# Encoder layer with retrieved experts: the low part of the one-hot weights on ScalarE in every second group, and a larger share for gathered rows

## Chip, cores and metric

The kernel runs on one core of a Trainium2 chip. The metric is the device time of one execution in microseconds (us). The engines carry their profile names: PE (TensorE), PEld (its weight loads), DVE (VectorE), ACT (ScalarE), POOL (GpSimd), SP (SyncE, which here issues transfers).

## What is computed

One layer of an encoder, 512 tokens of width 1024: an attention half and a recurrent half, then the retrieval of experts, then a gated embedding and a norm. The edit lies in the retrieval. Each token has 8 heads with 16 experts each, 128 of 16384, chosen by two short key searches; an expert is a row of `exp_u` and a row of `exp_v`:

```
idx, g = top 16 of the key sums, softmax of their scores    # per token and head
ue = exp_u[idx];  logits = einsum('td,tkd->tk', x, ue)
act = gelu(logits) * g
ve = exp_v[idx];  out = einsum('tk,tkd->td', act, ve)
```

## The kernel before, in words

The tokens form four tiles of 128. Three of them take the dense way: the products of all 16384 rows of `u` with the 384 tokens are formed on PE (the u product, 128 steps of 128 experts), gelu is applied, and the result is multiplied by a weight matrix that holds g at the chosen experts and zero elsewhere, and then with all rows of `v` (the v product, 128 steps again). The fourth tile takes the sparse way: for each of its tokens' 128 experts POOL gathers 128 rows (one for each token) from `u`, DVE forms dot products (L926), and later POOL gathers rows of `v` and DVE adds them to `h` (L933). That makes 256 gathers, called rows here.

Products run on 32-bit words split in a high part (by ACT, L89) and a low part (by DVE, L91), three matmuls for each product (L96 to L98). `row_load` loads and splits a block of rows, three blocks ahead of PE; `u_mm` (L655 on) forms 24 matmuls into one of two PSUM banks `psl`, which ACT empties with gelu (L660). In the v product six banks `acc` collect the sums.

The weight matrix is made by `build`, for one tile of 128 tokens, in groups of eight. For each group `hot` makes one-hot tiles on DVE: `o1` and `m2` compare a count from 0 to 127 with the first and second key's number (L830, one instruction of 1024 f16 elements each), and two multiplications put the weight on `m2`: `o2` with its high part and, in place, `m2` with its low part (L835). PE multiplies the two one-hot tiles of each token, high and low, into a bank `pg` (L855, 16 matmuls a group), ACT copies that to `sg` (L858), and every two groups `sg` is written to memory (`gd`, L860). A group's one-hot tiles are made one group ahead. For the second branch of `hot`, which the kernel before never takes since HOT_DVE is 4, ACT makes the same product in eight activations, one for each token, with the weight as the scale.

The order is set by hand. The loop over the 128 steps of the u product calls three generators after each step, each with a share: `top` (key search, tile by tile, the sparse tile first), `make` (the builds, a share of 0.5, a group costs 1.0) and `side` (the rows; one costs 1.15). `side` gets SIDE_1 while the first dense tile's indices are unknown, SIDE until all builds are done, then SIDE_2. At step 122 the builds that are left are forced, and `settle` opens the room of the v product and loads the first weights back from memory. In the loop of the v product the rows get BG_V at each step, or the last weights are prepared instead. Rows that are left come after the last step (`bg.run(1e9)`), together with `finish`: norm, turn, gate product and output of each tile (L1133 to L1165). The gathered rows' tile is the last to finish, since its `h` needs all rows. The order in which each engine gets its instructions follows from these calls and from a scheduler that interleaves what is ready. Every gather waits for the newest split of a block (`pace`).

Of the kernel before, what the change touches and what calls it, by code (L numbers as in the profile page):

```python
# [39 lines left out]
KEEP = 26  # L40
G_SCALE = 2.0 ** 14
RO_AT = [2, 1, 1, 1, 1, 1, 1, 0, 0, 1, 0, 0, 1, 0, 0, 1, 0, 0, 1, 1, 9]
TOP_FIRST, TOP_THEN, MAKE, SIDE_1, SIDE, BG_V, HOT_DVE, PREP, SIDE_2 = 2.2, 1.0, 0.5, 0.6, 1.2, 1.2, 4, 60, 2.1
LAST = 3
N_HOT = 13
N_AT = 15, 17, 17
# [1256 lines left out]
```

## Time and profile before

| | |
|---|---|
| median of 3 runs | 1504.44 us (1502.62 to 1505.04) |
| profiled execution | 1502.74 us, span 1501.0 us |
| PE, DVE, ACT, POOL busy | 98%, 84%, 49%, 29% of the span |
| u product | about 295 to 895 us |
| builds of the weights | about 400 to 866 us |
| v product | about 898 to 1437 us |

A row of a view gives an engine, a line of the kernel, the operation, the tiles (written <- read), the shape, and a count after x. Behind the bar stand busy us, mean ns of one, and the idle time of the engine just before, with what ended it. In a timeline the columns are start, duration, engine, line, operation; in brackets, idle time and what ended it. In a table of stretches the engines stand in the order PE, PEld, DVE, ACT, POOL, then the granted clock of PE (1.00 is full speed), the share of the DMA engines and GB/s.

### The profile page before, as it was taken

How to read it: one execution, taken by the hardware profiler on the slowest of the kernel's cores; microseconds unless marked ns; L12 is line 12 of the kernel's file. 1: busy time of each engine (PE TensorE's matmuls, PEld its weight loads, DVE VectorE, ACT ScalarE, POOL GpSimd, SP SyncE). 2: the span in 40 equal slices, each digit the busy share in tenths (PEclk: the TensorE clock that was granted, in tenths of full speed). 3: DMA queues.
4: the chain of work that ended last, by engine and by line, in shares of the span. 5: the costliest groups of instructions: out<-in, count | busy, mean ns of one | idle time of the engine just before them, and what ended most of it. 6: DMA issues, size and time to landing. Idle time of an engine off the chain costs nothing.

```text
span 1501.0 us, 22206 instructions
## 1 busy us (share of the span) xinstructions
PE 1464.1 (98%) x7907; PEld 1294.7 (86%) x7907; DVE 1257.0 (84%) x2481; ACT 741.1 (49%) x1059; POOL 428.6 (29%) x320
## 2 busy tenths in 40 slices
PE   8999999999899999999999989999999999999996
PEld 6887678899899999999999987888888888888875
DVE  7686987789999999999878757788887588878895
ACT  7974754354555654565455533333333453333345
POOL 0000000010223374235333344344443014344450
PEclk9999999999999999999999999999999999999998
DMA  7223022156789898889998799989999789999971
GB/s 257 61 94 127 15 86 88 43 195 229 239 294 335 285 347 327 305 296 345 370 330 300 266 321 340 321 300 328 360 373 359 248 280 351 366 353 357 322 227 64
DMA packets 169199, 394.21 MB, mean 263 GB/s; under 512 B 15360, under 2 KB 90880, under 8 KB 166016
## 3 DMA queue, kind: packets, MB, share of 16 engines
q1 hardware_dynamic: 112336, 207.52, 41.1%
q0 software_dynamic: 38464, 140.00, 26.4%
q10 hardware_dynamic: 18288, 45.27, 7.8%
q8 instruction: 62, 1.02, 0.3%
q14 instruction: 49, 0.40, 0.1%
HBM read 345.41 MB, written 47.32 MB: 262 GB/s over the span
## 4 chain that ended last, share of the span: by engine, by line
PE 66%; DVE 21%; ACT 4%; issue 4%; DMA 3%; SPq 1%; DVEq 0%; ACTq 0%
PE acc L98 11%; PE acc L97 11%; PE acc L96 11%; PE psl L96 6%; PE psl L97 6%; PE psl L98 6%; DVE rl L91 4%; PE pg L855 2%; DVE rr L926 2%; PE ps L96 2%; PE ps L98 2%; PE ps L97 2%; DVE h L933 1%; DMA r<-in_v_dram 1%; SPq L1000 1%
## 5 line engine op out<-in xcount | busy, mean ns | idle before, releaser
L89 ACT ACTIVATE rh<-r 128x1024 fp32r<-128x1024 f32 x256 | 270.8, 1059 | 423.1 <-PE psl L97 188.1
L91 DVE TENSOR_TENSOR rl<-r,rh 128x1024 fp32r<-128x1024 f32 x256 | 312.2, 1220 | 95.5 <-ACT rh L89 93.4
L96 PE MATMUL psl<-x2h,rh 128*128 128x384 f32 x1024 | 348.2, 340 | 7.4 <-ACT keep L660 5.0
L98 PE MATMUL psl<-x2h,rl 128*128 128x384 f32 x1024 | 344.3, 336 | 3.6 <-DVE rl L91 3.6
L97 PE MATMUL psl<-x2l,rh 128*128 128x384 f32 x1024 | 343.9, 336 | 0.0
L98 PE MATMUL acc<-rh,al 128*128 128x512 f32 x768 | 299.8, 390 | 1.1 <-DVE al L91 1.1
L96 PE MATMUL acc<-rh,ah 128*128 128x512 f32 x768 | 299.4, 390 | 0.7 <-ACT ah L89 0.7
L97 PE MATMUL acc<-rl,ah 128*128 128x512 f32 x768 | 299.4, 390 | 0.3 <-DVE rl L91 0.3
L894 POOL DMA_INDIRECT rr<-in_u_dram,qidx x84 | 123.0, 1465 | 382.0 <-DVE rl L91 180.7
L894 POOL DMA_INDIRECT rr<-in_v_dram,qidxv x82 | 150.8, 1839 | 187.7 <-DVE rl L91 163.9
L96 PEld LDWEIGHTS psl<-x2h,rh 128*128 128x128 f32 x1024 | 193.0, 189 | 8.9 <-ACT keep L660 5.3
L98 PEld LDWEIGHTS psl<-x2h,rl 128*128 128x128 f32 x1024 | 193.2, 189 | 4.6 <-DVE rl L91 4.5
L97 PEld LDWEIGHTS psl<-x2l,rh 128*128 128x128 f32 x1024 | 193.3, 189 | 0.0
L98 PEld LDWEIGHTS acc<-rh,al 128*128 128x128 f32 x768 | 144.5, 188 | 31.8 <-DVE al L91 1.9
L96 PEld LDWEIGHTS acc<-rh,ah 128*128 128x128 f32 x768 | 144.6, 188 | 31.2 <-ACT ah L89 1.1
L97 PEld LDWEIGHTS acc<-rl,ah 128*128 128x128 f32 x768 | 144.4, 188 | 30.6 <-DVE rl L91 0.7
L89 ACT ACTIVATE ah<-am 128x384 fp32r<-128x384 f32 x128 | 66.3, 518 | 94.9 <-DVE am L1057 61.5
L933 DVE SCALAR_TENSOR_TENSOR h<-rr,qg,h 128x1024 f32<-128x1024 f32 x82 | 104.9, 1279 | 3.7 <-DMA rr<-in_v_dram,qidxv 3.7
L926 DVE CUSTOM_DVE_ANT_0 rr<-rr,xn 128x1024 f32<-128x1024 f32 x84 | 102.1, 1217 | 6.0 <-DMA rr<-in_u_dram,qidx 6.0
L894 POOL DMA_INDIRECT xn<-in_u_dram,qidx x44 | 68.6, 1559 | 110.7 <-DVE rl L91 92.7
L894 POOL DMA_INDIRECT xn<-in_v_dram,qidxv x46 | 74.8, 1627 | 88.8 <-DVE rl L91 81.4
L858 ACT COPY sg<-pg 128x512 f32<-128x512 f32 x96 | 95.8, 1107 | 1.0 <-ACT sc L695 0.4
(342 smaller groups left out, 2275.5 us busy)
## 6 DMA issues: line engine op xcount, KB each, us to landing
r<-in_ut_dram SPq DMA_DIRECT2D x128, 512.0 KB, 4.8
r<-in_v_dram SPq DMA_DIRECT2D x128, 512.0 KB, 6.8
gd<-sg ACTq DMA_DIRECT2D x24, 1024.0 KB, 7.5
gc<-gd SPq DMA_DIRECT2D x128, 192.0 KB, 7.7
ld<-lg ACTq DMA_DIRECT2D x102, 192.0 KB, 5.0
lg<-ld SPq DMA_DIRECT2D x102, 192.0 KB, 6.3
w<-in_w_qkv_dram SPq DMA_DIRECT2D x12, 512.0 KB, 3.6
w<-in_w_out_dram SPq DMA_DIRECT2D x8, 512.0 KB, 3.8
```

What stands on the lines that cost most here:

```text
L89: nc.scalar.activation(hi, src, AF.Copy, scale=1.0 if scale is None else scale)
L91: return nc.vector.tensor_sub(lo, src, hi.bitcast(F32))
L96: nc.tensor.matmul(ps, lhsT=lh, rhs=rh, start=first, stop=False)
L97: nc.tensor.matmul(ps, lhsT=lh, rhs=rl, start=False, stop=False)
L98: nc.tensor.matmul(ps, lhsT=ll, rhs=rh, start=False, stop=last)
L855: nc.tensor.matmul(pg[:, i - q, :], lhsT=o1[:, i // 2, :, i % 2], rhs=o2[part][:, i // 2, :, i % 2], start=part == 0, stop=part == 1)
L858: nc.scalar.copy(sg[:, :, s0:s0 + 4].rearrange("p j t -> p t j"), pg)
L894: g = nc.gpsimd.indirect_dma_start(out=dst, out_offset=None, in_=table, in_offset=bass.IndirectOffsetOnAxis(ap=idx, axis=0))
L926: behind(nc.vector.tensor_tensor_reduce(rr, rr, xn[:, t, :], 1.0, 0.0, ALU.mult, ALU.add, act[:, k % 16:k % 16 + 1]))
L933: behind(nc.vector.scalar_tensor_tensor(h[:, t, :], rr, qg[:, t, k:k + 1], h[:, t, :], op0=ALU.mult, op1=ALU.add))
L1000: nc.sync.dma_start(gcs[-1][:, b0:b1], gd[b0:b1, :, j * TB:(j + JC) * TB].rearrange("b p (j t) -> p b j t", t=TB))
```

## The change

Two of the constants that steer the order get other values:

```diff
-TOP_FIRST, TOP_THEN, MAKE, SIDE_1, SIDE, BG_V, HOT_DVE, PREP, SIDE_2 = 2.2, 1.0, 0.5, 0.6, 1.2, 1.2, 4, 60, 2.1
+TOP_FIRST, TOP_THEN, MAKE, SIDE_1, SIDE, BG_V, HOT_DVE, PREP, SIDE_2 = 2.2, 1.0, 0.5, 0.6, 1.25, 1.2, 3, 60, 2.1
```

With HOT_DVE at 3 the condition in `hot` fails for the low part (part 1) of every odd group of eight tokens. There ACT makes the low part, in place in `m2`, in eight activations of 128 x 128 elements, each with a column of `gw` as scale; it has to wait for DVE's `o2`, which reads `m2` first.

```
if t0 // 8 % 2 * 2 + part < HOT_DVE:
    nc.vector.tensor_tensor(o, m2, along(2 + part, t0), op=ALU.mult)
else:
    for i in range(8):
        nc.scalar.activation(o[:, i // 2, :, i % 2], m2[:, i // 2, :, i % 2], AF.Copy,
                             scale=gw[:, part, t0 + i:t0 + i + 1])
```

SIDE goes from 1.2 to 1.25: the share of the rows in each step of the u product while builds are running.

## Rows read from the trace of the kernel before

**Rows 1.** The profile's page, its first part: busy us, share of the span and instructions of each engine.

```profile
span 1501.0 us, 22206 instructions
PE 1464.1 (98%) x7907; PEld 1294.7 (86%) x7907; DVE 1257.0 (84%) x2481; ACT 741.1 (49%) x1059; POOL 428.6 (29%) x320
```

**Rows 2.** The table of stretches: from and to, length, busy us of PE, PEld, DVE, ACT and POOL, granted clock, DMA share, GB/s.

```profile
400.00:550.00 150.00, 149.25 (x1022) 147.31 (x1022) 149.73 (x383) 83.21 (x110) 60.42 (x32) 1.00 0.88 305
550.00:700.00 150.00, 147.93 (x1013) 145.01 (x1013) 146.66 (x365) 82.74 (x110) 53.28 (x34) 1.00 0.89 318
700.00:860.00 160.00, 160.00 (x1089) 157.25 (x1088) 130.09 (x163) 81.86 (x107) 62.53 (x38) 1.00 0.90 322
860.00:900.00 40.00, 34.30 (x200) 33.21 (x199) 24.10 (x33) 15.32 (x22) 16.52 (x12) 0.91 0.93 318
```

**Rows 3.** PE's waits from 400 to 860 us, all of them: who waited for whom, us in total, times, longest.

```profile
PE psl L98 <- DVE rl L91: 2.1, 1, 2.1
PE ptt L809 <- DVE e L772: 0.4, 1, 0.4
PE psl L96 <- ACT lg L660: 0.3, 1, 0.3
```

**Rows 4.** PE's waits from 1430 us to the end, in the same columns.

```profile
PE turn L1141 <- DVE x L1135: 3.0, 1, 3.0
PE gate L96 <- DVE hl L91: 2.0, 1, 2.0
PE turn L1141 <- DVE h L1220: 1.2, 1, 1.2
```

**Rows 5.** Groups of instructions on DVE from 1438.7 to 1471 us: the rows added to h.

```profile
L933 DVE SCALAR_TENSOR_TENSOR h<-rr,qg,h 128x1024 f32<-128x1024 f32 x11 | 14.1, 1284 | 0.0
L933 DVE SCALAR_TENSOR_TENSOR h<-xn,qg,h 128x1024 f32<-128x1024 f32 x7 | 9.0, 1280 | 0.0
```

**Rows 6.** The timeline of all engines from the last row to the gate product of the last tile.

```profile
1469.22 1.28 DVE L933 SCALAR_TENSOR_TENSOR h<-xn,qg,h 128x1024 f32<-128x1024 f32 x1
...
1470.42 0.68 DVE L1153 TENSOR_TENSOR sg<-sg,pp 128x512 f32<-128x512 f32 x1
...
1472.83 0.39 PE L98 MATMUL gate<-wg,hl 128*128 128x512 f32 x1
...
1473.14 1.28 ACT L102 ACT_TABLE_LOAD   x1
...
1474.87 1.28 DVE L1135 SCALAR_TENSOR_TENSOR x<-h,sm,gains 128x1024 f32<-128x1024 f32 x1
...
1476.21 1.09 PE L1141 MATMUL turn<-ident,x 128*128 128x128 f32 x8 [3.00 <-DVE x L1135]
...
1479.30 0.79 PE L96 MATMUL gate<-wg,hl 128*128 128x512 f32 x1 [2.00 <-DVE hl L91]
```

**Rows 7.** The table of stretches again, after a wait of PE that ended at 672.8 us, and before and after its waits from 1473 to 1479.3 us; the last column but two is the granted clock.

```profile
672.80:690.00 17.20, 17.18 (x119) 16.86 (x120) 17.20 (x23) 6.60 (x9) 6.30 (x5) 1.00 0.88 302
...
1460.00:1473.00 13.00, 13.00 (x59) 10.61 (x57) 12.65 (x19) 8.42 (x14) 0.94 (x1) 1.00 0.36 121
...
1479.30:1487.00 7.70, 7.70 (x23) 6.16 (x24) 3.70 (x9) 1.89 (x5) 0.00 (x0) 0.67 0.37 136
```

**Rows 8.** Groups of instructions on DVE over the whole span: the multiplication that makes the low part.

```profile
L835 DVE TENSOR_TENSOR m<-m,gl 128x1024 f16<-128x1024 f16 x48 | 33.0, 687 | 0.6
```

**Rows 9.** Groups of instructions on ACT over the whole span.

```profile
L858 ACT COPY sg<-pg 128x512 f32<-128x512 f32 x96 | 95.8, 1107 | 1.0 <-ACT sc L695 0.4
...
L519 ACT ACTIVATE ugz<-pso,dng 128x512 f32<-128x512 f32 x4 | 2.8, 691 | 0.0
...
L518 ACT ACTIVATE ugz<-pso 128x512 f32<-128x512 f32 x4 | 2.4, 594 | 1.1 <-PE pso L98 1.1
L812 ACT ACTIVATE sT<-ptt 128x128 f16<-128x128 f32 x9 | 2.3, 275 | 1.6 <-PE ptt L809 1.0 <-PE psl L97 0.5
```

**Rows 10.** The timeline of all engines around an odd group of the first tile: ACT's split and evacuation, DVE's two multiplications and the low part of a row block, PE's next product.

```profile
442.94 1.05 ACT L89 ACTIVATE rh<-r 128x1024 fp32r<-128x1024 f32 x1
...
446.39 0.69 DVE L835 TENSOR_TENSOR o<-m,sT 128x1024 f16<-128x1024 f16 x1
...
447.51 0.47 ACT L660 ACTIVATE lg<-psl 128x384 f32<-128x384 f32 x1
...
447.72 1.22 DVE L91 TENSOR_TENSOR rl<-r,rh 128x1024 fp32r<-128x1024 f32 x1
...
447.77 0.42 PE L96 MATMUL psl<-x2h,rh 128*128 128x384 f32 x1
447.88 0.37 ACT L695 COPY sc<-pk 128x256 f32<-128x256 f32 x1
...
448.03 0.34 PE L97 MATMUL psl<-x2l,rh 128*128 128x384 f32 x1
448.20 0.34 PE L98 MATMUL psl<-x2h,rl 128*128 128x384 f32 x1
```

**Rows 11.** The same for a group of the third tile.

```profile
783.48 0.69 DVE L835 TENSOR_TENSOR o<-m,sT 128x1024 f16<-128x1024 f16 x1
...
784.50 1.05 ACT L89 ACTIVATE rh<-r 128x1024 fp32r<-128x1024 f32 x1
785.58 1.22 DVE L91 TENSOR_TENSOR rl<-r,rh 128x1024 fp32r<-128x1024 f32 x1 [0.69 <-ACT rh L89]
```

## The prediction

> **What bounds the kernel now.** I read the page's busy line first, then a table of stretches, then TensorE's waits in the two stretches that the edit touches, and only then single instructions. The busy line puts PE at 98% and DVE at 84%, with ACT at half [rows 1]. An average over stages says little, so the stretches come next [rows 2]. The edit works inside the first of the two large products (the u product), while one-hot weights are built: about 400 to 866 us. From 400 to 550 us DVE is busy 149.7 of 150 us and from 550 to 700 us 146.7 of 150; ACT is at 55%, and PE is as full as DVE. From 700 to 860 us the search for the top keys is over, DVE falls to 81%, and PE is busy without a break. So for 300 us PE and DVE are level, and the reader is to see which one makes the other wait. PE's waits tell: from 400 to 860 us it waited 2.1 us for DVE's low part of a row block, once, and 0.7 us for anything else [rows 3]. DVE is full there, but the three buffers ahead of PE take up its lateness. PE sets the pace, and at most 2.8 us of this stretch can be won by making DVE's load lighter.
>
> The end is different. From 1430 us on PE waits 3.0 us for the normalised last tile, then 2.0 us for its low part, after 1.2 us earlier [rows 4]. The cause is the expert rows of that tile: between 1438.7 and 1471 us DVE adds 18 of them to h (11 and 7) and has no idle time [rows 5]. The last ends at 1470.4, square and root follow, the normalised tile starts at 1474.87, PE can turn it at 1476.21 although its last matmul of the other tiles had started at 1472.83, and the gate product of the last tile starts at 1479.30 [rows 6]. It also pays in clock: from 1479.3 to 1487 us the granted clock is 0.67, after 1.00 before the two waits, so part of that product runs at 1.2 instead of 2.4 GHz [rows 7]. From 900 us up to there nothing of this edit runs except the same rows at an unchanged rate.
>
> **The change, part by part.** (1) *VectorE's relief.* There are 3 tiles of 128 tokens, so 48 groups of eight, 24 of them odd. In those, one DVE multiplication of 0.687 us goes [rows 8]: 24 x 0.687 = 16.5 us of DVE time. On the path it is worth the waits it removes. By that wait, which ended at 672.8 us, twelve of the second tile's groups are begun, six of them odd: 6 x 0.69 = 4.1 us, less one extra row of 1.2 us, is more than the 2.1 us by which DVE was late. I take **-2.1 us**; bounds 0 and -2.8.
>
> (2) *ScalarE's eight activations.* The trace has no such instruction (128 x 128, f16 to f16, every second element, the scale read from a column). The nearest are the f16 copy of the same size, 0.275 us, and a copy of 512 elements with a column as scale beside a square of 512 without one: 0.691 against 0.594 us, +0.10 [rows 9]. One costs about 0.375 us and starts about 0.10 us before its predecessor ends (the evacuation of 0.47 us at 447.51 is followed by a start at 447.88 [rows 10]). So eight take 8 x 0.275 + 0.1 = 2.3 us. If the write with gaps costs what it does in the copy to sg, 1.107 us for 512 elements [rows 9], each is (1.107 - 0.594) x 128 / 512 = 0.13 us dearer and a group takes 3.3 us. 24 groups cost 55 to 80 us of ACT, which has 67 + 67 + 78 us free in the three stretches up to 860 us [rows 2]. ACT's total is therefore covered; its order is not. The eight wait for DVE's high part, and behind them in ACT's queue stand the split that feeds the next row block and the evacuation that frees PE's PSUM bank. While DVE is late, ACT inherits the lateness: at 446.39 DVE makes the high part of an odd group's weights, and the low part of the row block that ACT split from 442.94 to 443.99 follows only at 447.72, 3.7 us late [rows 10]. PE alternates between two banks, so an evacuation may be late by about one product of 24 matmuls, 24 x 0.17 = 4.1 us [rows 10], less the 1.5 us that split and evacuation take: some 2.6 us. Where DVE is not late (785 us: its low part starts 0.03 us after the split ends [rows 11]) the eight end 2 us after the split would start, inside that slack, and cost nothing. In the late stretch the eight cost between nothing (behind split and evacuation) and, at the example, 447.1 + 2.3 + 0.5 = 449.9 against a bank wanted at 447.8: 2 us (ahead of them). A stall gives DVE the time back, and the edit takes 3.7% of its work away, so the lateness should not be rebuilt often. I take one such stall, **+2.0 us**; bounds 0 and 16 of them, 32.
>
> The Trainium skill (ScalarE: Activation LUTs, section What ACT_TABLE_LOAD costs) gives 186 ns plus 0.833 ns an element, 93 ns for a column operand and 93 ns of overlap. By it eight would take 2.4 us instead of 2.3, and the sum would not move by more than 0.1 us a stall.
>
> (3) *No new table.* The copy function runs on ACT in this stretch already, between the same neighbours, so no table load is added.
>
> (4) *The larger share.* SIDE counts from the step where the first tile's indices are known (step 24) to the end of the builds (forced at step 122): 98 steps x 0.05 = 4.9, at 1.15 a row four rows more. Counting the code's shares through, 122 rows are placed by the end of the u product, 235 by the end of the main loop of the v product and 18 at the end; the trace's 18 agrees [rows 5]. After the edit it is 126, 239 and 14. The four rows cost DVE 4 x 1.2 = 4.8 us in the u product, covered by the 16.5 us, and four gathers there move 2 MB more in a stretch that carries some 310 GB/s [rows 2]; the rows land ahead and hide. At the end 4.8 us of DVE work is missing. The turn becomes possible at 1476.2 - 4.8 = 1471.4, before PE's other gate matmuls are over at about 1473, so the 3.0 us wait goes. The 2.0 us for the split probably stays, since the turn's place in PE's order is behind those matmuls; then PE's next wait is that one. The single wait of 2.1 us [rows 3], which ended at 672.8 us, left the clock at 1.00 [rows 7], so the slow stretch goes as well: 7.7 x (1 - 0.67) = 2.5 us. I take **-5.5 us**; bounds 0 (other DVE work keeps its place ahead of the last tile) and -7.5 (the split hidden too).
>
> (5) *Handover between the products.* From 860 to 900 us PE is idle 5.7 us while the last weights go to memory and come back [rows 2]. The last group is odd, but its low part is made a group ahead; I cost it at nothing. If that cover is gone, 2.3 us are added.
>
> Sum: -2.1 + 2.0 - 5.5 = **-5.6 us**. The profiled execution took 1502.74 us (span 1501.0 and 1.74 around it), which makes 1497.1; the median of the runs is 1.7 us higher, so I state 1504.4 - 5.6 = **1498.8 us**. About 0.2%, 3 us, is what a measurement here can tell from none.
>
> **The rivals.**
> *ScalarE passes VectorE's lateness on to PE* (slower). Place: the 16 odd groups of the first two tiles, built between 400 and 710 us while DVE is full [rows 2]. Price: 2 us for each in which the eight stand ahead of evacuation and split; with half of the groups 16 us, and the u product's 2.1 us not won. At the end -5.5 still holds: 1504.4 + 16 - 5.5 = 1515. From five such groups on (10 - 5.5 us) the kernel is slower by more than can be told from none. For it: DVE is full, and the example's 2 us. Against it: every stall lets DVE catch up, and from 700 us on there is slack. Beside it stands a rule of the Trainium skill (ScalarE: Activation LUTs, Rules for kernel authors) to make plain multiplications on VectorE, not on ScalarE. This trace agrees on engine time, 2.3 against 0.69 us, but not on which engine has time to spare. Chance 0.23.
>
> *The gains are eaten or never come* (no change). Either the last tile's chain keeps its end, held by something other than the rows (the backlog of 2 us of other DVE work and the table load of 1.28 us between the last row and the root [rows 6]), or two or three stalls in ACT cost what the end gives: 1504.4 - 5.6 + 5.5 = 1504. The edit would then only move DVE time that nobody waited for. For it: 98% of PE's time is busy and DVE's 16.5 us lie under it. Against it: the end's 3.0 us wait names DVE, and DVE has no gap before. Chance 0.22.
>
> **How the numbers follow.** Likeliest, 0.55: 1498.8, own range 1494.8 (end -7.5, no stall) to 1501.4. No change, 0.22: 1501.4 to 1507.4. Slower, 0.23: 1515, spread from 1507.4 up to 32 us above. The range for 8 in 10 runs from 1494 to 1515: it leaves out about a tenth above and less below. Faster 0.55, same 0.22, slower 0.23.
>
> **What would show it.** In the profile after: DVE's 48 low multiplications become 24, ACT gains 192 instructions of about 0.37 us on the same line; DVE busy between 400 and 700 us below 290 of 300; PE's wait on the low part of a row block gone and its waits for ACT's evacuation there at 0 to 4 us in all; 14 rows at the end instead of 18; PE's turn without the 3.0 us wait, and the granted clock near 1.00 in the last gate product. I am wrong if PE waits for ACT more than 5 us in the u product, if the last turn waits as long as before, or if the v product changes its length.

## The result: slower by 1.2%, and where the 22 us lie

The changed kernel takes **1521.99 us** (median of 4 runs, 1520.3 to 1524.86) against 1504.24 us of the kernel before in the same session (1502.62 to 1505.04): a ratio of 1.0121, interval 1.0106 to 1.0136. The forecast was 1498.8 us; the range ended at 1515. The profiled execution took 1524.86 us, with a span of 1523.0 us. First the busy line of its page, which answers to [rows 1].

```profile
span 1523.0 us, 22304 instructions
PE 1473.9 (97%) x7907; PEld 1298.5 (85%) x7907; DVE 1242.6 (82%) x2457; ACT 794.1 (52%) x1251; POOL 398.6 (26%) x320
```

The edit itself is there as described: 24 instructions fewer on DVE, 192 more on ACT, 14 us less DVE and 53 us more ACT. PE does the same 7907 matmuls in 10 us more busy time. So the loss isn't more work; PE waits, and runs for a while at a lower clock. The table of stretches (from and to, length, PE, PEld, DVE, ACT, POOL, granted clock, DMA share, GB/s) answers to the first three of [rows 2].

```profile
400.00:550.00 150.00, 147.60 (x1008) 144.41 (x1007) 144.07 (x373) 97.90 (x167) 51.09 (x32) 1.00 0.85 298
550.00:700.00 150.00, 148.59 (x1010) 145.87 (x1009) 145.20 (x362) 101.16 (x174) 63.97 (x35) 1.00 0.90 324
700.00:860.00 160.00, 153.50 (x1039) 150.47 (x1037) 119.33 (x148) 97.12 (x167) 58.98 (x40) 0.98 0.90 315
```

The stretch in which DVE was full got a little worse. But 6.5 us of PE time are lost in the third, where DVE has slack. A table by stage, from the start times of PE's matmuls in the profiled executions, shows both places. Stages: up to the first matmul of the u product (step 0); from the start of its step 1 to that of 23, from 23 to 93 and from 93 to 122; from there to the first matmul of the v product; the v product, first to last matmul; from there to the end. Step 0, some 47 us in every run, has no column. The runs e1 to e11 are those of the section on experiments.

| us | first | 1–23 | 23–93 | 93–122 | to v | v product | end | span |
|---|---|---|---|---|---|---|---|---|
| before | 247.6 | 99.5 | 334.0 | 135.5 | 35.0 | 538.5 | 64.0 | 1501.0 |
| after | 248.7 | 101.2 | 335.6 | **144.3** | 34.5 | **552.0** | 59.8 | 1523.0 |
| e1, ScalarE alone | 248.8 | 99.1 | 338.2 | 135.6 | 35.0 | 542.4 | 63.8 | 1509.8 |
| e2, larger share alone | 248.2 | 99.2 | 339.9 | 140.9 | 32.3 | 554.7 | 59.7 | 1521.8 |
| e3, loads earlier | 248.5 | 101.1 | 334.6 | **147.1** | 33.3 | 536.7 | 56.9 | 1505.0 |
| e4, order of buffers | 248.3 | 100.7 | 334.4 | 135.6 | 32.5 | **550.9** | 59.7 | 1509.0 |
| e5, both | 249.5 | 100.6 | 334.7 | 135.6 | 32.3 | 535.3 | 56.9 | 1491.8 |
| e6, as e5, all on DVE | 247.4 | 99.4 | 335.4 | 136.6 | 30.9 | 540.3 | 56.9 | 1493.7 |
| e7, share 1.29 | 245.8 | 100.8 | 336.1 | 135.6 | 28.5 | 544.3 | 56.2 | 1494.0 |
| e8, as e7, all on DVE | 248.1 | 100.8 | 340.5 | 135.6 | 31.8 | 545.0 | 56.2 | 1504.8 |
| e9, before with loads later | 248.3 | 98.9 | 333.6 | 135.5 | 34.0 | **554.6** | 67.4 | 1519.2 |
| e10, before, one buffer free | 248.1 | 101.1 | 332.9 | 135.5 | 33.8 | **561.0** | 64.2 | 1523.5 |
| e11, no gathers ahead | 247.3 | 99.1 | 336.8 | 135.5 | 32.7 | 545.8 | 56.9 | 1501.0 |

Of 22.0 us, 8.8 are lost at step 93 of the u product and 13.5 in the v product; the end gives 4.2 back, and 3.9 are spread over the rest. The medians differ by 17.8 us only: the changed kernel's profiled execution was the slowest of its four, and e1's the slowest of ten, 5.8 us above its median. Executions of one kernel scatter (20 of the kernel before, in the session of e1, took 1498.2 to 1509.6 us), so a difference of 2 or 3 us in a single cell is not told from scatter; the 8.8 and the 13.5 us come back in other runs.

PE's waits name the engines (who waited for whom, us in total, times, longest); from 400 to 880 us, to be held against [rows 3]:

```profile
PE psl L98 <- DVE rl L91: 6.9, 3, 6.2
PE psl L96 <- ACT lg L660: 1.5, 1, 1.5
PE ptt L809 <- ACT sT L812: 1.4, 1, 1.4
```

From 900 to 1430 us, where PE waited for nothing in the kernel before from 930 us on:

```profile
PE psl L96 <- ACT keep L660: 4.5, 1, 4.5
PE psp L96 <- ACT wg L89: 4.2, 1, 4.2
PE acc L98 <- DVE al L91: 3.8, 4, 2.6
PE acc L96 <- ACT ah L89: 1.9, 2, 1.6
PE acc L97 <- DVE rl L91: 1.3, 2, 0.8
```

**First place, step 93.** DVE and ACT are named, but a wait's name is only its last link. The timeline of the changed kernel around 736 us, POOL and DVE (start, duration; in brackets idle time and what ended it):

```profile
718.14 0.93 POOL L894 DMA_INDIRECT xn<-in_u_dram,qidx  x1 [0.30 <-issue]
...
724.32 1.23 DVE L926 CUSTOM_DVE_ANT_0 rr<-rr,xn 128x1024 f32<-128x1024 f32 x1 [4.93 <-DMA rr<-in_u_dram,qidx]
...
727.10 0.93 POOL L894 DMA_INDIRECT xn<-in_u_dram,qidx  x1 [4.31 <-DMA xn<-in_u_dram,qidx]
...
736.75 1.23 DVE L926 CUSTOM_DVE_ANT_0 xn<-xn 128x1024 f32<-128x1024 f32 x1 [10.06 <-DMA xn<-in_u_dram,qidx]
737.90 1.22 DVE L91 TENSOR_TENSOR rl<-r,rh 128x1024 fp32r<-128x1024 f32 x1
```

DVE stands still 10.06 us for a gathered row, with the low part of a row block behind it, on which PE waits its 6.2 us. Behind that wait, from 738.5 to 743 us, the granted clock is 0.51, some 2.2 us more: 8.4 of the 8.8 us. `rows` hands each gather the next place of a ring: four `rr` buffers and tile 0 of `xn`; once the key search is over, tiles 1 and 2 of `xn` as well. The place is the entry's number in the list modulo the ring's size (the list counts the gelu entries too), and the size goes from 5 to 7 in mid-run. Gather 84 (expert 49) gets tile 0 (84 mod 5 = 4). The key search ends as row 83 is treated. From there gather 88 gets tile 0 too (88 mod 7 = 4), and it is asked for at once, ahead of the reading of row 84. The gather at 727.10 thus overwrites what was fetched at 718.14, and DVE's dot product, which waits for the newest write, gets there 10 us late. By the same count the kernel before makes the switch four rows earlier in the list, at row 79, and the row in tile 0 is then that one itself: none waits there.

That is an error in the result too, and not only a loss of time: for each token of the sparse tile, the changed kernel, e2 and e3 form the dot product of expert 49 with the `u` row of expert 53. Transfers and instructions are as many, so the times can still be compared, but the edit cannot be kept without turning the order of the buffers as in e4.

**Second place, the v product.** At its step 60 the last weights are prepared: `prepare` takes its `w` buffers from the same four `rr` and loads them through POOL's queue. POOL's timeline of the kernel before there:

```profile
1143.07 1.68 POOL L894 DMA_INDIRECT xn<-in_u_dram,qidx  x1 [2.77 <-DVE rl L91]
1144.76 0.61 POOL L1103 DMA_DIRECT2D w<-in_pT_dram  x1
...
1148.37 0.59 POOL L1106 DMA_DIRECT2D w<-in_w_proj_dram  x1
```

The timeline of the changed kernel in the same place, all engines:

```profile
1156.76 1.68 POOL L894 DMA_INDIRECT rr<-in_v_dram,qidxv  x1 [2.40 <-DVE rl L91]
...
1230.50 1.68 POOL L894 DMA_INDIRECT xn<-in_v_dram,qidxv  x1 [72.06 <-DVE rl L91]
...
1234.23 1.22 DVE L926 CUSTOM_DVE_ANT_0 rr<-rr,xn 128x1024 f32<-128x1024 f32 x1
1234.58 1.68 POOL L894 DMA_INDIRECT xn<-in_v_dram,qidxv  x1 [2.40 <-DVE rl L91]
1236.26 0.60 POOL L1103 DMA_DIRECT2D w<-in_pT_dram  x1
...
1240.37 0.58 POOL L1106 DMA_DIRECT2D w<-in_w_proj_dram  x1
...
1244.18 0.63 ACT L89 ACTIVATE wg<-w 128x512 fp32r<-128x512 f32 x1 [7.16 <-DMA w<-in_pT_dram]
...
1248.76 1.22 PE L96 MATMUL psp<-wg 128*128 128x512 f32 x2 [4.24 <-ACT wg L89]
```

Before, the gathers in flight stood in the `xn` tiles and two `rr` were free. Shifted by four rows, all four `rr` hold rows not yet read, and while `prepare` has the turn no row is read. POOL is idle 72 us: the loads have no buffer, and the next gather, which ends the idle time at 1230.50 and waits for a block's split (`pace`), comes in the code only behind the turn of `prepare`. The first load goes out 91 us later than before (1236.26 against 1144.76), right after a row in `rr` was read at 1234.23. The products that need these weights crowd into steps 81 and 82 of the v product, where they had been spread over 64 to 67. ACT, in order, waits 7.16 us for a load, PE waits for ACT, and the granted clock follows. The table of stretches of the changed kernel shows it, in the columns above:

```profile
1235.00:1244.00 9.00, 9.00 (x42) 7.44 (x41) 3.85 (x7) 1.48 (x2) 4.14 (x4) 1.00 1.04 386
1244.00:1249.00 5.00, 0.76 (x4) 0.34 (x3) 4.12 (x7) 3.28 (x6) 0.57 (x1) 0.91 0.63 215
1249.00:1256.00 7.00, 7.00 (x19) 5.35 (x20) 4.55 (x6) 2.92 (x4) 2.11 (x4) 0.58 0.91 286
```

PE is idle 4.2 of 5 us, and then runs 7 us at a granted clock of 0.58, mostly at 1.2 instead of 2.4 GHz. Over the whole v product PE is idle 11.5 of 552.0 us, against 2.2 of 538.5 before: 9.3 us of waits. The clock takes 7 x (1 - 0.58) = 2.9 us here; in the kernel before it took 5 x (1 - 0.66) = 1.7 us, from 917 to 922 us. Together that is some 10.5 of the 13.5 us; the other 3 are not assigned.

### The profile page after: what moved, and what is told of

It reads as the page before. It is cut to its first block, busy times and chain, and to the rows that moved or that the text cites. A ratio compares the mean times of both kernels' runs of the same rounds, so it can differ in the third digit from the quotient of the medians.

```text
span 1523.0 us, 22304 instructions
## 1 busy us (share of the span) xinstructions
PE 1473.9 (97%) x7907; PEld 1298.5 (85%) x7907; DVE 1242.6 (82%) x2457; ACT 794.1 (52%) x1251; POOL 398.6 (26%) x320
## 4 chain that ended last, share of the span: by engine, by line
PE 48%; DVE 19%; issue 14%; DMA 9%; ACT 5%; POOL 4%; SPq 1%; DVEq 0%; POOLq 0%; ACTq 0%
PE acc L98 6%; PE acc L97 6%; PE acc L96 6%; PE psl L98 5%; PE psl L96 5%; PE psl L97 5%; DVE rl L91 4%; DMA r<-in_v_dram 4%; POOL rr L894 3%; DVE rr L926 2%; PE ps L96 2%; PE ps L98 2%; PE ps L97 2%; DMA xn<-in_u_dram,qidx 1%; SPq L1000 1%
## 5 line engine op out<-in xcount | busy, mean ns | idle before, releaser
L894 POOL DMA_INDIRECT rr<-in_u_dram,qidx x84 | 116.2, 1383 | 376.8 <-DVE rl L91 174.2
L894 POOL DMA_INDIRECT rr<-in_v_dram,qidxv x82 | 138.9, 1694 | 169.3 <-DVE rl L91 146.2
L96 PEld LDWEIGHTS acc<-rh,ah 128*128 128x128 f32 x768 | 144.6, 188 | 33.8 <-ACT ah L89 3.7
L894 POOL DMA_INDIRECT xn<-in_v_dram,qidxv x46 | 71.3, 1550 | 178.8 <-DVE rl L91 165.9
L91 DVE TENSOR_TENSOR al<-am,ah 128x384 fp32r<-128x384 f32 x128 | 71.0, 554 | 43.0 <-ACT ah L89 41.4
```

The source lines that it names most:

```text
L91: return nc.vector.tensor_sub(lo, src, hi.bitcast(F32))
L96: nc.tensor.matmul(ps, lhsT=lh, rhs=rh, start=first, stop=False)
L894: g = nc.gpsimd.indirect_dma_start(out=dst, out_offset=None, in_=table, in_offset=bass.IndirectOffsetOnAxis(ap=idx, axis=0))
```

## Experiments

Ratios are to the kernel before on the same chip. Two theories stood at the start: S, the first rival of the prediction (ScalarE passes VectorE's lateness on to PE); B, the shifted rows collide in their buffers. The cut diffs show the values of SIDE, BG_V, HOT_DVE and PREP; those of e1 to e3, e7 and e8 start from the changed kernel, that of e6 from e5, those of e9 and e10 from the kernel before. First the two halves of the change alone.

**e1: ScalarE alone.**

```diff
- ... 1.25, 1.2, 3, 60 ...
+ ... 1.2, 1.2, 3, 60 ...
```

> Half the change: HOT_DVE 3 with SIDE left at 1.2. Theory B (the buffers of the gathered rows: the larger share shifts the rows by four, so that all four gather buffers hold rows that wait when the last weights are to be loaded, and one buffer is used again before its row is read when the key search ends): the u product loses no 8.6 us at its step 93 and the v product stays at the 538 us of before, so the time is that of the kernel before within 5 us, 1500 to 1507 us, with 18 rows at the end. Theory S (ScalarE hands VectorE's lateness to PE): the u product keeps at least 8 us of the loss, 1512 us or more.

Measured: 1505.86 us, ratio 1.0008 (0.9990 to 1.0026): no difference. What S describes does happen once, in the u product of the profiled execution, which was the slowest of the ten. ACT's timeline:

```profile
710.09 1.61 ACT L838 ACTIVATE m<-m,gw 128x128 f16<-128x128 f16 x5 [9.59 <-DVE o L835]
711.57 0.47 ACT L660 ACTIVATE lg<-psl 128x384 f32<-128x384 f32 x1
```

The eight wait 9.59 us for DVE's high part, the evacuation stands behind them, and PE waits 3.7 us for it; from 712 to 719 us the granted clock is then 0.58, another 7 x 0.42 = 2.9 us. That is the mechanism of S in its place, but one stall and not the eight that were priced at 16 us. It is not the cause of the loss. The v product, expected at 538 us, took 542.4.

**e2: the larger share alone.**

```diff
- ... 1.25, 1.2, 3, 60 ...
+ ... 1.25, 1.2, 4, 60 ...
```

> The other half: SIDE 1.25 with HOT_DVE left at 4. Theory B: the loss is here, above all in the v product (some 552 us from its first to its last matmul instead of 538), and the end gives some 4 us back: 1512 to 1526 us. Theory S: without ScalarE's eight activations there is no loss, the end's 4 us are won, 1498 to 1503 us.

Measured: 1520.58 us, 1.0100 (1.0073 to 1.0127). Nearly all of the loss comes with one constant that moves four rows; its stages lose in the same two places (DVE's wait for the row in tile 0 is 12.49 us here and begins ahead of step 93, so two columns share that loss). S falls, B stands.

**e3: the loads four steps earlier**, so that the gathers in flight are at another point of the ring.

```diff
- ... 1.25, 1.2, 3, 60, 2.1
+ ... 1.25, 1.2, 3, 56, 2.1
```

> The kernel after with PREP at 56 instead of 60: the last weights are prepared four steps earlier in the v product, when two of the four gather buffers are free, as in the kernel before. Theory B: the v product is back at 537 to 541 us, the four steps that form the embedding product lie together again, 10 to 14 us come back: 1507 to 1513 us. Theory S: nothing in the v product depends on ScalarE's eight activations, which are over by then, but four steps earlier or later should not matter either: 1519 to 1525 us.

Measured: 1503.17 us, 0.9996 (0.9970 to 1.0022). POOL's timeline has the loads early again:

```profile
1137.08 1.67 POOL L894 DMA_INDIRECT xn<-in_u_dram,qidx  x1 [2.40 <-DVE rl L91]
1138.75 0.62 POOL L1103 DMA_DIRECT2D w<-in_pT_dram  x1
...
1142.87 0.59 POOL L1106 DMA_DIRECT2D w<-in_w_proj_dram  x1
```

The v product is back at 536.7 us, and PE has no wait from 1000 to 1430 us; the loss at step 93 stays. The median lies 4 us below the range that was expected; the profiled execution, 1506.74 us, lies at its lower end.

**e4: the extra buffers in another order**, so that tile 0 comes last after the switch.

```diff
-            extra = [0, 1, 2] if top.done else [0]
+            extra = [1, 2, 0] if top.done else [0]
```

> The kernel after with the three extra gather buffers taken in the order 1, 2, 0 once the key search is done: then no buffer is given out again before its row is read at that switch. PREP stays at 60. Theory B: the 8.6 us at step 93 of the u product shrink to under 2, the v product keeps its loss: 1512 to 1517 us. Theory S: the u product's loss is ScalarE's and stays: 1519 to 1525 us.

Measured: 1512.85 us, 1.0071 (1.0042 to 1.0101). Its timeline at the place that cost 10 us:

```profile
715.71 0.93 POOL L894 DMA_INDIRECT xn<-in_u_dram,qidx  x1 [0.30 <-issue]
...
720.68 0.94 POOL L894 DMA_INDIRECT xn<-in_u_dram,qidx  x1 [0.31 <-issue]
...
723.85 1.23 DVE L926 CUSTOM_DVE_ANT_0 xn<-xn 128x1024 f32<-128x1024 f32 x1 [0.17 <-DMA xn<-in_u_dram,qidx]
```

Row 49 is read after its own gather with 0.17 us of waiting, the stage is at 135.6 us as before, and the v product keeps its loss. The two collisions are independent: e3 removes the second alone, e4 the first alone.

**e5: both edits.** e3's and e4's lines together.

> The kernel after with both mends: PREP at 56, and the extra gather buffers in the order 1, 2, 0. Theory B: neither loss is left, the u product is within 3 us of before, the v product 536 to 539 us, the end 57 to 60 us after the last matmul of the v product: 1492 to 1500 us, faster than before. If the two losses had a common cause beside the buffers: 1505 us or more.

Measured: 1496.24 us, **0.9962** (0.9943 to 0.9981): faster than both kernels. How much of this gain belongs to the edit and how much to the two mends isn't shown, since no run has the mends without the larger share; 7.1 of the 9.2 us between the two profiled executions are won at the end, where fewer rows are left. Its waits of PE from 930 us to the end are these:

```profile
PE turn L1141 <- DVE h L1220: 1.2, 1, 1.2
PE turn L1141 <- DVE sm L1161: 0.5, 1, 0.5
```

**e6: both edits, with all low parts on DVE**, to price ScalarE's part without collisions.

```diff
- ... 1.25, 1.2, 3, 56 ...
+ ... 1.25, 1.2, 4, 56 ...
```

> The same two mends with HOT_DVE back at 4, so VectorE makes all low parts. If ScalarE's share is worth anything, it is because VectorE is full while four more rows are placed: then this is 2 to 6 us slower than the kernel with ScalarE's share, 1497 to 1505 us. If ScalarE's activations only cost, it is 2 to 5 us faster, 1490 to 1495 us.

Measured: 1498.15 us, 0.9979 (0.9961 to 0.9997). The interval overlaps e5's: the difference, 0.17% for ScalarE's part at this share, isn't told from nothing.

**e7 and e8: a still larger share, 1.29**, with ScalarE's part and without it; loads and order of buffers as in the changed kernel.

```diff
- ... 1.25, 1.2, 3, 60 ...
+ ... 1.29, 1.2, 3, 60 ...      (e7)
+ ... 1.29, 1.2, 4, 60 ...      (e8)
```

> The kernel after with SIDE 1.29 instead of 1.25 and nothing else. By the count of the code's shares eight rows more than before are placed in the u product, two of the four gather buffers are free when the last weights are to be loaded, no buffer is given out early, and 10 rows are left at the end. Theory B: a still larger share costs nothing of what 1.25 cost, v product 536 to 541 us: 1490 to 1503 us. If it is the amount of rows in the u product that hurts, and not where they stand in the ring of buffers, it is slower than 1.25 was: 1522 us or more.

> SIDE 1.29 with HOT_DVE back at 4: the same rows and buffers as the run with 1.29, all low parts on VectorE. If ScalarE's share pays because VectorE is full, this is 2 to 8 us slower than that run, some 1500 to 1508 us; if it only costs, 1492 to 1498 us; if it is worth nothing that can be told, 1498 to 1502 us.

Measured: e7 1500.19 us, 0.9981 (0.9967 to 0.9995); e8 1507.97 us, 1.0026 (1.0013 to 1.0038). So more rows than in the changed kernel take less time, which no theory of the rows' work as such (DVE, DMA, POOL) allows: it is their phase. The v product of e7 is 544.3 us and not the 536 to 541 expected; it starts 6.5 us sooner behind the u product than before (28.5 against 35.0 us), so that both together are no longer. And at this share ScalarE's part is worth 0.45%, where the two intervals don't touch (each against the kernel before on its own chip); in the profiled executions e8 takes 340.5 us for steps 23 to 93, e7 336.1.

**e9: the kernel before with its loads four steps later.** If B holds, the old kernel loses the same way without any part of the change.

```diff
- ... 1.2, 1.2, 4, 60, 2.1
+ ... 1.2, 1.2, 4, 64, 2.1
```

> The kernel before with PREP at 64 instead of 60 and nothing else: no activations of ScalarE, no larger share. By the count all four gather buffers hold waiting rows when the last weights are to be loaded. Theory B: the v product grows by 10 to 16 us although the rows are the same, 1514 to 1522 us. Otherwise: 1501 to 1507 us.

Measured: 1520.90 us, 1.0114 (1.0083 to 1.0144). POOL's timeline repeats the long wait and the late loads:

```profile
1237.05 1.68 POOL L894 DMA_INDIRECT xn<-in_v_dram,qidxv  x1 [72.35 <-DVE rl L91]
...
1242.53 0.61 POOL L1103 DMA_DIRECT2D w<-in_pT_dram  x1
...
1246.63 0.59 POOL L1106 DMA_DIRECT2D w<-in_w_proj_dram  x1
```

**e10: the same with three steps**, where by the count of the ring one buffer is free.

```diff
- ... 1.2, 1.2, 4, 60, 2.1
+ ... 1.2, 1.2, 4, 63, 2.1
```

> The kernel before with PREP at 63: by the count three of the four gather buffers hold waiting rows and one is free when the last weights are to be loaded (two at 60, none at 64). Theory B with one free buffer enough to start: the four loads go through one buffer one after the other, a loss below 8 us, 1501 to 1511 us. If the loss depends on how many buffers are free, it lies between those of 60 and 64: 1508 to 1515 us.

Measured: 1525.16 us, 1.0139 (1.0123 to 1.0155), above what was expected. POOL's and PE's timeline:

```profile
1162.86 0.59 POOL L1103 DMA_DIRECT2D w<-in_pT_dram  x1
...
1172.31 0.55 POOL L1106 DMA_DIRECT2D w<-in_w_proj_dram  x1 [8.86 <-DVE wg L91]
...
1185.17 0.53 POOL L1106 DMA_DIRECT2D w<-in_w_proj_dram  x1 [5.22 <-DVE wg L91]
...
1192.03 0.80 PE L96 MATMUL psp<-wg 128*128 128x512 f32 x1 [6.61 <-ACT wg L89]
```

I had taken one free buffer for half the harm of none. It does more: the loads go early but one by one through the single buffer, each waiting until DVE has split the one before, and PE waits in the middle of them. The place of the cause was right, its price not.

**e11: e4, with no rows gathered ahead while the loads are due.** The step of the loads stays at 60.

```diff
-            while n < len(items) and n < i + GBUFS + len(extra) - 1:
+            while n < len(items) and n < (i + 1 if hold else i + GBUFS + len(extra) - 1):
...
+        if i == PREP - 5:
+            hold.append(1)
...
+            if prep.done:
+                hold.clear()
```

> The changed kernel with the order of the extra buffers turned (as in e4_extra), the weights' loads where they were (step 60 of the v product), and one thing more: from five steps ahead of them until they are all out, rows are not gathered ahead, so that the four buffers they share with the weights are free when the loads ask for them. Theory of the shared buffers: the loads go out one right after the other near 1140 to 1170 us, POOL has no wait of tens of us, and the v product is 535 to 545 us, as in e5_both and not 551 as in e4_extra; the time is 1492 to 1504 us, though with the same number of gathered rows or a few fewer. Rival (more rows simply cost the v product its time, through DMA or POOL): 550 us and 1509 to 1516 us.

Measured: 1502.50 us, 0.9994 (0.9972 to 1.0016), against 1.0071 of e4. POOL's timeline:

```profile
1124.62 0.61 POOL L1103 DMA_DIRECT2D w<-in_pT_dram  x1
...
1149.85 0.53 POOL L1124 DMA_DIRECT2D w<-in_w_gate_dram  x1 [3.83 <-DVE am L1057]
...
1196.22 0.53 POOL L1124 DMA_DIRECT2D w<-in_w_gate_dram  x1 [45.84 <-DVE wg L91]
```

The time is as theory B expected, the details only in part: the loads begin at once, but the last four wait 45.8 us for a buffer, and the v product takes 545.8 us, at the edge of what was expected and 10 us more than in e5. That long wait isn't what e11 loses by: the kernel before has such a wait too, 26.32 us ahead of the load at 1193.36, and behind 1150 us PE waits 1.6 us in all. Of PE's waits from 930 to 1430 us, 4.1 us, the other 2.5 lie between 1120 and 1150, where the loads come in; from 1143 to 1150 DVE is busy 7.00 of 7 us and the granted clock is 0.52. That points to the loads that come all at once, which no run tests.

## Why the prediction was wrong, step by step

**The step that failed is (4), the larger share**: "the rows land ahead and hide", with the sentence ahead of it that from 900 us on nothing of the edit runs "except the same rows at an unchanged rate". The rate was unchanged, as forecast; the rows' place in the ring was not. I priced four rows by DVE's time and by DMA traffic, and did not ask in which buffers they land, nor who else draws from these. That is +8.8 us at step 93 and +13.5 in the v product. e4 takes the first away, e3 the second, and e9 makes the second in the kernel before. All that was needed stood in `rows` and `prepare`. I had counted the rows through the code's shares, and the same count modulo 5 and 7 would have shown both.

*(1) VectorE's relief, -2.1.* The wait of [rows 3] that ended at 672.8 us is gone, and DVE's busy time from 400 to 700 us fell from 296.4 to 289.3, as forecast ("below 290"). But steps 1 to 93 took 3.3 us more than before, and 3.8 more in e1, so no gain shows there. Of the 3.3 us 1.7 lie ahead of step 23, where the edit does nothing yet (e10, unchanged up to there, has the same 101.1 us); in e1 the stall of step (2) is larger than the 3.8.

*(2) ScalarE's activations, one stall, +2.0.* Groups of instructions of the changed kernel on ACT and DVE (count | busy us, mean ns | idle before and what ended it), and, from its timeline, one group of eight:

```profile
L838 ACT ACTIVATE m<-m,gw 128x128 f16<-128x128 f16 x192 | 63.4, 429 | 39.2 <-DVE o L835 33.9 <-DVE rl L91 3.6 <-issue 0.2
L835 DVE TENSOR_TENSOR m<-m,gl 128x1024 f16<-128x1024 f16 x24 | 16.5, 687 | 0.4
```

```profile
749.42 2.49 ACT L838 ACTIVATE m<-m,gw 128x128 f16<-128x128 f16 x8 [2.15 <-DVE o L835]
```

Eight take 2.49 us where I took 2.3, one 0.429 where I took 0.375. The estimate from the page that I cited, the Trainium skill (ScalarE: Activation LUTs, What ACT_TABLE_LOAD costs), was 2.4 for eight, and the trace is nearer to it. ACT stands idle 33.9 us ahead of them for DVE, as the step said it would, and PE pays for little of it: a wait of 1.5 us in the changed kernel, 3.7 in e1. The one stall, +2.0, is about right for the changed kernel; in e1 it came to 6.6 us, since the step left out the clock behind the wait (2.9 us).

*(3) No new table.* Right: no load of a table was added with these instructions, which run between the same neighbours.

*(4), the end, -5.5.* The rows are as forecast, 14 instead of 18, and the sum nearly so, but not its parts. From 1430 us on PE waits once (first line, to be held against [rows 4]), and that is not the last tile, whose turn starts without idle time (second line):

```profile
PE turn L1141 <- DVE x L1135: 2.2, 1, 2.2
```

```profile
1499.53 1.03 PE L1141 MATMUL turn<-ident,x 128*128 128x128 f32 x8
```

The wait of 3.0 us is gone, as the step said. So is the 2.0 us for the split, which it kept. What is left, 2.2 us at 1465.80, is an earlier tile's turn right behind the v product, where the kernel before waited 1.2. In all 6.2 us of waits became 2.2: 4.0 of the table's 4.2 us. (The end of the last row, which the prediction puts at 1470.4, is 1470.5 by [rows 6]; nothing hangs on it.) The rows of the last tile:

```profile
L933 DVE SCALAR_TENSOR_TENSOR h<-rr,qg,h 128x1024 f32<-128x1024 f32 x8 | 10.3, 1283 | 0.1
L933 DVE SCALAR_TENSOR_TENSOR h<-xn,qg,h 128x1024 f32<-128x1024 f32 x6 | 7.7, 1278 | 0.0
```

Those are the groups on DVE from 1465.5 us to the end, to be held against [rows 5]; the stage gave 4.2 us here and 7.1 in e3 and e5, where no wait of 2.2 us is left. The clock, 0.67 in [rows 7], is 1.00 in the stretch that holds the last gate product; but from 1466.5 to 1470 us, behind the wait that is left, it is 0.51, so 3.5 x 0.49 = 1.7 of the 2.5 us that the step took for the clock are lost again there.

```profile
1499.50:1515.00 15.50, 15.50 (x96) 13.90 (x94) 9.37 (x18) 10.40 (x20) 0.00 (x0) 1.00 0.19 69
```

*(5) Handover.* 34.5 against 35.0 us: nothing, as taken.

**The rivals.** The first rival, theory S, ended on the right side for the wrong reason: e1 has its stall once, at 6.6 us and not 16. "The gains are eaten" fits e1 (1.0008). The mechanism that decided was not among the rivals, and the range, built from those that were, ended 7 us below the result. Of the things listed as proof of error, the last one, a v product that changes its length, was the one that came true.

The rule of the Trainium skill that the prediction weighed (ScalarE: Activation LUTs, Rules for kernel authors: multiplications belong on VectorE) holds here for engine time: eight activations take 2.49 us, the one multiplication 0.687. As advice it differs from the measurement at the larger share, where the activations still win 0.45% (e7 against e8). The likely reason, argued and not shown by itself, is that VectorE is busy 293 of 300 us there and ScalarE 164 (e8, 400 to 700 us). At the share of this change the runs tell no difference (e5 against e6).

## What to carry to other kernels

A knob that shifts how many items are done by some step shifts the phase of every ring of buffers behind it: count, modulo the ring's size, what is in flight where the ring changes size and where a second user draws from it, before pricing the items' work. A wait of tens of us on a queue that is 26% busy (here 72 us on POOL) is worth following to what should have run in it and to the buffer which that lacked, since the wait that PE shows names only the last link (ScalarE's split, 4.2 us). A buffer that is given out before it is read costs more than time: it changes what is computed. And a change that loses may hold a gain: with the two collisions taken out the same edit is 0.4% faster than the kernel before, though no run shows what the two mends alone would give there.

## What was not expected of the hardware

One short idle stretch of PE in the v product (4.2 of 5 us) was followed by 7 us at a granted clock of 0.58, as was the single wait of 3.7 us in e1, whereas the single wait of 2.1 us in the kernel before had left it at 1.00 [rows 7]. And an ACT instruction of 128 x 128 elements with gaps of one element in input and output and a column as scale took 0.429 us, against 0.275 for the copy of the same size without them [rows 9].
